# Ordering a DEPTH-2 encoder trunk by estimated times instead of counted half-chunk ticks

## The chip, the cores and the metric

The kernel runs on one core of one Trainium2 chip. The metric is device microseconds for one execution of the whole program, as the median of several executions.

## The reference

Two layers of a pre-norm encoder on 256 tokens of width 2048, all in fp32, batch 1. In each layer one input projection of the normalised stream feeds four branches, whose outputs are gated, lifted to 2048 columns, merged by sigmoid gates and passed through an output projection into a residual add:

```
h  = rmsnorm(x)                       # 256 x 2048
p  = h @ W_in                         # u, za, q/k/v and gates of each branch, 4 x 2048 merge gates
A  = s5(u): two scans (forward, backward) of 48 groups x 64 complex states,
     y = gelu(y);  y = y * sigmoid(y @ W_glu + b_glu)
B  = gated DeltaNet (bidirectional, chunks of 64, short convolution)
C  = grouped-query attention with 2-D rotary positions
M  = cross-attention into 256 memory tokens, rmsnorm(mem) @ W_km, W_vm
x  = x + (sum over br of sigmoid(gate_br) * ((br * silu(z_br)) @ W_br)) @ W_out
```

A final rmsnorm ends the trunk.

## The kernel before

**The weight stream.** All weights lie in `wpack` as chunks of 128 x 1024 fp32 (512 KB), 720 of them, in the order in which they are used. SP loads a chunk into `raw` (3 buffers), ACT rounds it to fp32r (`hi`, 3 buffers), DVE makes the rest, `lo` = `raw` - `hi` (3 buffers), and TensorE (PE) multiplies each with the activations, which are split in the same way, into `acc` (PSUM, 2 buffers). A chunk is 24 matmuls of 256 columns (kind T, `acc<-xT,hi`) or 12 of 512 columns (kind N, `acc<-hi,xT`). A run of chunks that fills one `acc` is a unit: `km`, `vm` (memory keys and values), `glu`, `out` and so on; `acts` are its activations (`xT` from the normalised stream, `memT` from memory, `sy` from the S5 output, `mT` from the merged branches).

**The branch work** (softmax, DeltaNet, the S5 scan, norms, transposes) is written as generators, called fibers. PE uses four PSUM tiles `bank` for it, and 13 tiles `scr` of 128 x 512 serve as scratch. Everything is emitted by one Python program and keeps that order on each engine: the order of emission is the order of execution. Nothing is reordered afterwards.

**What sets the order.** `run_unit` calls `tick` after each half chunk. A fiber yields the number of ticks to let pass before it goes on, for instance 6 between the issue of a load and its first use. `tick` runs fibers by rank while two counters of estimated backlog, one for DVE and one for ACT, are under `LIMIT`. The emptying of `acc` is put in `deferred` and is run first in a tick. Chunks are asked for by count: at the start of chunk n, `pump_split` emits `hi` and `lo` up to n+2, and `pump_raw` the loads up to n+4, whether a `raw` buffer is free by then or not; SP then waits at that load, with all later loads behind it.

**S5, where the prediction's terms lie.** `s5_fiber` has three stages in each layer. `chunk_sums` (12 blocks): 2 loads `scr<-Bd` of 256 KB each per block, which PE multiplies with `s5u`. A scan of 31 steps on DVE (`s5s`). `outputs` (12 blocks): 4 loads of 256 KB each per block, 2 `scr<-Wd` that DVE adds, and 2 `scr<-Cd` that go to PE with the sum. The result goes to DRAM (`Yd`), is read back as `s5y`, passes through gelu on ACT and DVE and is split into `sy`, which the `glu` units need. All these loads are on SP's queue, among the `raw` loads.

Helpers record the line of the helper: L240 is any ACT or DVE call, or a PE call on a `bank`; L418 is the stream's matmul, L372 the `raw` load.

Of the kernel before, what the change touches and what calls it, by code (L numbers as in the profile page):

```python
# [2 lines left out]

# [5 lines left out]
F32 = mybir.dt.float32  # L9
# [65 lines left out]
def layer_units(layer):  # L75
    """The weight stream of one layer, in the order in which the tensor engine takes it."""
# [78 lines left out]
def pack_small(inp):  # L155
    """Gains, biases and the like, per layer, one value or row per partition."""
# [20 lines left out]
def pack_s5(inp):  # L177
    """Per layer and partition (direction, state): a, log step, b and c; and d as diagonal blocks."""
# [12 lines left out]
def shape_consts():  # L191
    """Constants that follow from the shapes: identity, rotary angles, masks of the two directions."""
# [20 lines left out]
class Bank:  # L213
    """A set of equal tiles handed out and taken back in program order."""

    def __init__(self, tiles):
        self.free = list(tiles)

    def put(self, *tiles):
        self.free += tiles  # L220


class Meter:
# [5 lines left out]
    def __init__(self, eng, load, names, per, fixed):  # L229
        self._e, self._load, self._names, self._per, self._fixed = eng, load, names, per, fixed  # L230

    def __getattr__(self, name):
        f = getattr(self._e, name)

        def call(*args, **kw):
            o = kw.get("in_", kw.get("out", args[0] if args else None))
            if o is not None and name != "dma_start":
                for e in self._names:
                    self._load[e] += self._fixed + self._per * o.free_size()
            return f(*args, **kw)  # L240
        return call


class Builder:
    # microseconds of each engine per tick, and the backlogs between which the branches' work goes on
    DRAIN = {"V": 1.1, "S": 1}
    LIMIT = {"V": 2.125, "S": 2}
    FLOOR = {"V": 0.7, "S": 0.8}
    # memory attention, DeltaNet, attention and S5 by layer, and the preparation of S5
    RANK = ((3, 2, 4, 5), (5, 2, 4, 3))  # L250
    PREP_RANK = (3.5, 2.5)
    # ticks between the work of another engine and the tensor engine's use of it
# [46 lines left out]
    # A tick is half a chunk. A fiber yields the number of ticks to let pass before it goes on; 0 marks a place to pause.  # L299
    # Where an engine needs what another one makes, a tick in between keeps it from waiting for it in its queue.  # L300
    def spawn(self, gen, rank=None):
        """Of the fibers that can go on, the one with the lowest rank does; its own fibers get its rank."""
        self.fibers.append([self.tick_no, gen, self.rank if rank is None else rank])
        self.fibers.sort(key=lambda f: f[2])

    def wait(self, key):
        while key not in self.ready:
            yield 1

    def take(self, bank, n):  # L310
        while len(bank.free) < n:
            yield 1
        out, bank.free = bank.free[:n], bank.free[n:]
        return out
# [4 lines left out]
    def take_now(self, bank, n):  # L319
        while len(bank.free) < n:  # L320
            self.tick()
        out, bank.free = bank.free[:n], bank.free[n:]
        return out

    def tick(self):
# [3 lines left out]
        todo, self.deferred = self.deferred, []  # L329
        for due, f in todo:  # L330
            if due > self.tick_no:
                self.deferred.append((due, f))
                continue
            f = f() if callable(f) else f
            n = "end" if f is None else next(f, "end")
            if n != "end":
                self.deferred.append((self.tick_no + n, f))
        while all(self.load[e] < self.LIMIT[e] for e in self.load):
            f = next((f for f in self.fibers if f[0] <= self.tick_no), None)
            if f is None:  # L340
                break
            self.rank = f[2]
            try:
                f[0] = self.tick_no + next(f[1])
            except StopIteration:
                self.fibers.remove(f)
            self.rank = 0

    def need(self, key):
        guard = 0  # L350
        while key not in self.ready:
            self.tick()
            guard += 1
            assert guard < 100000, f"never ready: {key}"

# [1 line left out]
    def stream_setup(self):  # L357
# [18 lines left out]
    def pump_split(self, i):  # L376
        while self.next_split <= min(i, len(self.queue) - 1):
            n, w = self.next_split, self.queue[self.next_split]
            self.pump_raw(n)
            r = self.raw.pop(n)  # L380
            hi = self.hip.tile([128, CW], F32R, tag="hi", name="hi")
            lo = self.lop.tile([128, CW], F32R, tag="lo", name="lo")
            self.S.activation(out=hi[:, 0:w], in_=r[:, 0:w], func=AF.Copy)
            self.V.tensor_tensor(out=lo[:, 0:w], in0=r[:, 0:w], in1=hi[:, 0:w].bitcast(F32), op=ALU.subtract)
            self.split[n] = (hi, lo)
            self.next_split += 1

    def run_unit(self, u, act, nt=NT):
        """One unit of the stream: its product with the activations, in two banks of PSUM."""
        nc = self.nc  # L390
        acc = self.psa.tile([128, 2, 512], F32, tag="acc", name="acc")
        k = 0
        for j in range(u.nch):
            n = u.ch0 + j
            self.pump_split(n + self.AHEAD)
            self.pump_raw(n + self.AHEAD + 2)
            hi, lo = self.split.pop(n)
            todo, late, half = [], [], 6 if u.kind == "N" else 12
# [16 lines left out]
            todo += late  # L415
            for i, (kk, o, w, x, start, stop) in enumerate(todo):
                self.need(u.key + (kk // 4,))
                nc.tensor.matmul(o, w, x, start=start, stop=stop)  # L418
                if i == half - 1 or i == len(todo) - 1:
# [4 lines left out]
    def hi_lo(self, hi, lo, src, scale=None):  # L424
        """hi + lo = scale * src, each in the 12 bits that one pass of the tensor engine carries."""
# [8 lines left out]
    def hi_lo_later(self, *args):  # L434
        """hi_lo with a tick between the two engines."""
# [9 lines left out]
    def rsqrt(self, out, in_, mul, eps=EPS, p=-0.5):  # L445
        """out = (in_ * mul + eps) ** p on GpSimd, for a few columns."""
# [1180 lines left out]
```

## Time and profile before

| | us |
|---|---|
| median of 3 runs | 2333.71 |
| lowest and highest | 2330.08, 2336.09 |
| span of the profiled execution | 2329.0 |
| PE busy in it | 2261.9 (97%) |
| DVE, ACT busy | 1704.0 (73%), 1245.9 (53%) |
| DMA | 523.39 MB, mean 225 GB/s |

The span is that of one profiled execution. It lies 4.7 us under the median of the three runs. Of the span, PE sits idle for 2329.0 - 2261.9 = 67.1 us; a busy PE can still run at half its clock, which the column PEclk of the profile shows as a mean granted clock under 1.

### The profile page before, as it was taken

The page shows a single profiled execution, that of the slowest core. Times are in us where ns is not written, and L with a number is a line of the kernel's source. Part 1 is how long each engine was busy: PE and PEld are TensorE (multiplying, and loading weights), DVE is VectorE, ACT ScalarE, POOL GpSimd, SP SyncE. Part 2 cuts the span into 40 slices and gives each one's busy share as a digit, 9 for nine tenths or more (in the row PEclk, how much of TensorE's full clock was granted, in tenths as well). Part 3 has the DMA queues.
Part 4 walks back from the last instruction along what each step waited for, and adds up shares of the span by engine and source line. Part 5 has one row for each costly group of instructions (what it writes and reads, how often), then busy time and mean ns, then how long its engine had stood idle before and what let it go on. Part 6 is the DMA issues. An engine that isn't in the chain of part 4 may idle for free.

```text
span 2329.0 us, 38887 instructions
## 1 busy us (share of the span) xinstructions
PE 2261.9 (97%) x14684; PEld 1960.0 (84%) x14684; DVE 1704.0 (73%) x2824; ACT 1245.9 (53%) x2176; POOL 88.3 (4%) x153
## 2 busy tenths in 40 slices
PE   6999999999999999799999999999999999999997
PEld 6888978988988788697789987889888878888886
DVE  6788878858768955689688856888547895566564
ACT  6655564565564355555655554665646445554443
POOL 0000000000010000000000001000000000000000
PEclk9999999999999999999999999999999999999999
DMA  6677678745776488678776795656468558877674
GB/s 222 226 240 249 213 248 276 228 153 182 212 241 194 145 305 303 185 246 276 250 239 197 237 302 178 223 180 198 157 194 271 186 175 283 286 230 245 231 239 146
DMA packets 245133, 523.39 MB, mean 225 GB/s; under 512 B 59320, under 2 KB 111032, under 8 KB 244304
## 3 DMA queue, kind: packets, MB, share of 16 engines
q1 hardware_dynamic: 218400, 471.41, 63.1%
q10 hardware_dynamic: 21952, 36.80, 4.4%
q0 software_dynamic: 4592, 12.69, 1.6%
q8 instruction: 115, 1.88, 0.3%
q14 instruction: 74, 0.61, 0.1%
HBM read 468.21 MB, written 65.18 MB: 229 GB/s over the span
## 4 chain that ended last, share of the span: by engine, by line
PE 87%; DVE 5%; DMA 3%; ACT 3%; issue 1%; SPq 0%; ACTq 0%; POOL 0%; POOLq 0%; DVEq 0%
PE acc L418 78%; PE bank L240 9%; DVE lo L240 2%; DMA raw<-wpack 2%; ACT hi L240 1%; DVE scr L240 1%; DVE dnx L240 1%; ACT scr L240 0%; DVE s5s L240 0%; DMA xm<-x 0%; DMA s5y<-Yd 0%; SPq L1243 0%; ACT gt L240 0%; DMA oTA<-gt 0%; DMA Rb<-Rd 0%
## 5 line engine op out<-in xcount | busy, mean ns | idle before, releaser
L240 DVE TENSOR_TENSOR lo<-raw,hi 128x1024 fp32r<-128x1024 f32 (+1 forms) x720 | 873.5, 1216 | 528.1 <-ACT hi L240 512.5
L240 ACT ACTIVATE hi<-raw 128x1024 fp32r<-128x1024 f32 (+1 forms) x720 | 757.7, 1055 | 712.8 <-PE acc L418 368.6
L418 PE MATMUL acc<-hi,xT 128*128 128x512 f32 x2432 | 633.5, 398 | 3.0 <-ACT hi L240 2.4
L418 PEld LDWEIGHTS acc<-hi,xT 128*128 128x128 f32 x2432 | 447.0, 189 | 98.6 <-issue 5.6
L418 PE MATMUL acc<-xT,hi 128*128 128x256 f32 x3392 | 460.6, 287 | 8.1 <-DVE xT L240 5.6
L418 PEld LDWEIGHTS acc<-xT,hi 128*128 128x128 f32 x3392 | 427.6, 193 | 20.2 <-issue 8.4
L418 PE MATMUL acc<-lo,xT 128*128 128x512 f32 x1216 | 327.3, 391 | 2.6 <-DVE lo L240 2.5
L418 PEld LDWEIGHTS acc<-lo,xT 128*128 128x128 f32 x1216 | 228.2, 188 | 54.1 <-DVE lo L240 4.8
L418 PE MATMUL acc<-xT,lo 128*128 128x256 f32 x1696 | 238.8, 284 | 0.0
L418 PEld LDWEIGHTS acc<-xT,lo 128*128 128x128 f32 x1696 | 219.4, 192 | 0.1
L240 ACT ACTIVATE scr<-bank 128x128 f32<-128x128 f32 (+6 forms) x324 | 105.2, 335 | 140.9 <-PE bank L240 111.0
L418 PE MATMUL acc<-hi,y 128*128 128x512 f32 x640 | 163.2, 395 | 0.0
L418 PEld LDWEIGHTS acc<-hi,y 128*128 128x128 f32 x640 | 117.6, 188 | 25.3 <-issue 1.0
L418 PE MATMUL acc<-hi,mT 128*128 128x512 f32 x512 | 131.3, 397 | 0.0
L240 DVE TENSOR_TENSOR dnx<-dnx 32x30 f32<-32x30 f32 (+9 forms) x360 | 114.6, 318 | 10.4 <-DVE dnx L240 0.5
L418 PEld LDWEIGHTS acc<-hi,mT 128*128 128x128 f32 x512 | 95.3, 190 | 19.5 <-issue 0.4
L418 PE MATMUL acc<-lo,y 128*128 128x512 f32 x320 | 85.8, 390 | 0.0
L240 DVE TENSOR_TENSOR scr<-scr,scr 128x512 f32<-128x512 f32 (+4 forms) x132 | 77.4, 590 | 3.6 <-DMA scr<-s 1.1
L240 DVE SCALAR_TENSOR_TENSOR hT<-acc,small,hT 128x254 f32<-128x254 f32 (+1 forms) x144 | 69.3, 481 | 3.9
L418 PEld LDWEIGHTS acc<-lo,y 128*128 128x128 f32 x320 | 60.1, 188 | 12.8
L418 PE MATMUL acc<-lo,mT 128*128 128x512 f32 x256 | 68.6, 390 | 0.0
L240 PE MATMUL bank<-consts,scr 128*128 128x128 f32 x388 | 62.3, 274 | 5.3 <-DVE memT L240 5.2
(186 smaller groups left out, 2036.8 us busy)
## 6 DMA issues: line engine op xcount, KB each, us to landing
raw<-wpack SPq DMA_DIRECT2D x714, 512.0 KB, 4.2
Bd<-scr ACTq DMA_DIRECT2D x48, 256.0 KB, 4.4
Cd<-scr SPq DMA_DIRECT2D x48, 256.0 KB, 4.6
Wd<-Kd SPq DMA_DIRECT2D x32, 384.0 KB, 6.8
scr<-Bd SPq DMA_DIRECT2D x48, 256.0 KB, 5.5
scr<-Wd SPq DMA_DIRECT2D x48, 256.0 KB, 4.9
scr<-Cd SPq DMA_DIRECT2D x48, 256.0 KB, 5.5
Rb<-Rd SPq DMA_DIRECT2D x48, 128.0 KB, 4.5
```

The lines of the kernel that those rows point to most:

```text
L240: return f(*args, **kw)
L418: nc.tensor.matmul(o, w, x, start=start, stop=stop)
```

## The change

The counted ticks and the backlog counters go. A `Clock` keeps for each engine an estimated time at which it is free and, for each piece of a tile, when it was last written and read; each call is wrapped (`Engine`) and advances it by an estimated duration. Fibers go on when the estimated end of what they did last lies at least `MARGIN` before the estimated time of PE. `tick` is called after every 3 (N) or 6 (T) matmuls. Emptying `acc`, loading a `z` unit's branch output and loading its gate become fibers of rank -1. `raw` loads are emitted only when their buffer is estimated free, and `hi` and `lo` when their source is estimated there. The estimated landing of a load takes no account of other loads in flight: `dma` computes it from its own size only. The branch code itself (which instructions, which tiles, which queues) is unchanged, but for the words that declare a result ready.

```diff
 class Builder:
-    DRAIN = {"V": 1.1, "S": 1}
-    LIMIT = {"V": 2.125, "S": 2}
-    FLOOR = {"V": 0.7, "S": 0.8}
+    LIMIT = 2.0
+    LIMIT_EVAC = 4.0
+    MARGIN = 0.25
...
+    def dma(self, eng, out, in_):
...
+        kb = max(out.size(), 1) * 4 / 1024
+        self.t[eng] = dep + (0.5 if eng == "G" else 0.06)
+        land = dep + 2.0 + kb / 200.0
+        self.mark(land, W, R)
...
     def tick(self):
-        self.tick_no += 1
-        for e in self.load:
-            self.load[e] = max(-self.FLOOR[e], self.load[e] - self.DRAIN[e])
...
-        while all(self.load[e] < self.LIMIT[e] for e in self.load):
-            f = next((f for f in self.fibers if f[0] <= self.tick_no), None)
...
+        self.pump_raw(self.ahead, False)
+        self.splits()
+        seen = set()
+        while True:
+            now, back = self.time(), self.backlog()
+            f = next((f for f in self.fibers if f not in seen and f.t + self.MARGIN <= now
+                      and back < (self.LIMIT_EVAC if f.rank < 0 else self.LIMIT)), None)
+            if f is None:
+                return
+            self.cur, self.rank, self.clock.end = f, max(f.rank, 0), 0.0
+            n = next(f.gen, "end")
+            f.busy = max(f.busy, self.clock.end)
...
     def pump_raw(self, i, force=True):
         while self.next_raw <= min(i, len(self.queue) - 1):
+            old = self.next_raw - 3
+            if not force and (old in self.raw or self.gone.get(old, 0.0) > self.time() + 0.3):
+                return
...
+    def empty(self, u, acc, l, last):
+        if last is not None:
+            yield from self.wait(("emptied", last))
+        f = getattr(self, "evac_" + u.name)(u, acc, l)
+        if f is not None:
+            yield from f
+        u.emptied = True
+        yield 1
+        self.mark(("emptied", u))
```

How this moves instructions is read from the compiled order of both kernels. SP's queue at the S5 outputs of layer 0, before (`raw` is the weight stream; one row is one load, or several when it ends in a count):

```order
L372 DMA raw<-wpack 128x1024 x21
L1302 DMA scr_81<-Wd 128x512
L1303 DMA scr_87<-Wd 128x512
L1305 DMA scr_86<-Cd 128x512
L1305 DMA scr_91<-Cd 128x512
L372 DMA raw<-wpack 128x1024 x3
L1302 DMA scr_82<-Wd 128x512
L1303 DMA scr_80<-Wd 128x512
L1305 DMA scr_89<-Cd 128x512
L1305 DMA scr_79<-Cd 128x512
L372 DMA raw<-wpack 128x1024 x3
```

and after, at the same place (here and below L361 is the helper's line in place of L240 and L372):

```order
L361 DMA raw<-wpack 128x1024
L361 DMA scr_91<-Wd 128x512
L361 DMA scr_88<-Wd 128x512
L361 DMA scr_80<-Cd 128x512
L361 DMA scr_84<-Cd 128x512
L361 DMA raw<-wpack 128x1024
L361 DMA scr_81<-Wd 128x512
L361 DMA scr_85<-Wd 128x512
L361 DMA scr_90<-Cd 128x512
L361 DMA scr_79<-Cd 128x512
L361 DMA scr_87<-Wd 128x512
L361 DMA scr_80<-Wd 128x512
```

Before, 2 or 3 `raw` loads stand between the four loads of one block and those of the next; now there are 0 to 2. From the first `scr<-Wd` of the layer to the last `scr<-Cd`, 48 loads of 256 KB, there are 10 `raw` loads in all. The `chunk_sums` stage has the same: 24 loads `scr<-Bd` with 7 `raw` loads among them.

ACT at the S5 result `sy`, before; `gt<-acc,hbg` empties the first `glu` unit:

```order
L240 ACTIVATE scr_80<-s5y 128x512
L240 ACTIVATE scr_84<-scr_84 128x512
L240 ACTIVATE scr_83<-scr_83 128x512
L240 ACTIVATE scr_80<-scr_80 128x512
L240 ACTIVATE sy<-s5y 128x2x256 x3
L1057 DMA scr_90<-s 128x144
L240 ACTIVATE hi<-raw 128x1024
L240 ACTIVATE hi<-raw 128x512
L240 ACTIVATE hi<-raw 128x1024
L240 ACTIVATE gt<-acc,hbg 128x256 x2
```

and after:

```order
L361 ACTIVATE hi<-raw 128x1024
L361 ACTIVATE sy<-s5y 128x2x256
L361 ACTIVATE scr_84<-scr_84 128x512
L361 ACTIVATE sy<-s5y 128x2x256
L361 ACTIVATE gt<-acc 128x512
L361 ACTIVATE hi<-raw 128x1024 x2
L361 ACTIVATE y<-gt 128x2x256
L361 ACTIVATE sy<-s5y 128x2x256
L361 ACTIVATE hi<-raw 128x1024 x2
```

Before, three `hi` splits stand between `sy` and the first emptying of a `glu` unit. After, more than twenty do: `sy` is made while the units ahead of `glu` still run.

POOL at the start of layer 1's memory, before:

```order
L1532 DMA xm<-x 128x2x512 x4
L535 DMA memtok<-mem 128x2048 x2
L1190 MEMSET scr_82 128x256
L1549 DMA x_97<-xm 128x2x512
L448 TENSOR_SCALAR nstat<-nstat 128x2
```

and after:

```order
L361 DMA xm<-x 128x2x512 x4
L361 DMA x_97<-xm 128x2x512
L361 DMA memtok<-mem 128x2048 x2
L361 MEMSET scr_84 128x256
L361 TENSOR_SCALAR nstat<-nstat 128x2
```

The load of `memtok` now stands behind a store of the first finished columns of `x`, and its user on ACT follows three chunks of PE work later, where before it was four.

## Rows read from the trace of the kernel before

**Rows 1.** The page: busy time of each engine, and the chain that ended last.
```profile
PE 2261.9 (97%) x14684; PEld 1960.0 (84%) x14684; DVE 1704.0 (73%) x2824; ACT 1245.9 (53%) x2176; POOL 88.3 (4%) x153
...
PE 87%; DVE 5%; DMA 3%; ACT 3%; issue 1%; SPq 0%; ACTq 0%; POOL 0%; POOLq 0%; DVEq 0%
```

**Rows 2.** By 50 us: busy us (count) of PE, PEld, DVE, ACT, POOL; PEclk, DMA share, GB/s.
```profile
0.00:50.00 50.00, 30.80 (x214) 29.46 (x215) 33.10 (x88) 31.23 (x62) 1.10 (x6) 0.93 0.63 223
50.00:100.00 50.00, 47.10 (x296) 42.17 (x296) 37.19 (x56) 34.27 (x65) 1.41 (x4) 0.97 0.73 239
...
750.00:800.00 50.00, 45.17 (x315) 35.83 (x313) 47.43 (x125) 19.57 (x34) 0.00 (x0) 0.97 0.45 144
900.00:950.00 50.00, 44.35 (x256) 35.12 (x254) 30.34 (x37) 22.18 (x32) 0.00 (x0) 0.99 0.90 284
950.00:1000.00 50.00, 43.22 (x241) 37.37 (x242) 35.57 (x79) 31.79 (x50) 1.82 (x3) 0.91 0.54 172
1050.00:1100.00 50.00, 47.81 (x253) 39.01 (x252) 44.90 (x62) 23.70 (x40) 1.76 (x3) 1.00 0.80 270
1100.00:1150.00 50.00, 47.62 (x237) 38.47 (x236) 34.03 (x53) 30.63 (x61) 4.50 (x8) 0.97 0.81 278
1900.00:1950.00 50.00, 47.40 (x330) 38.73 (x329) 38.78 (x84) 23.58 (x49) 2.11 (x2) 0.97 0.60 203
```

**Rows 3.** PE's timeline at the stalls: start, us, group [idle before it <-releaser].
```profile
787.65 1.23 PE L240 MATMUL bank<-dnx,scr 128*128 128x128 f32 x8 [2.29 <-DVE scr L240]
788.57 3.67 PE L418 MATMUL acc<-hi,xT 128*128 128x512 f32 x8
...
954.01 0.58 PE L418 MATMUL acc<-sy,hi 128*128 128x256 f32 x1 [9.66 <-ACT sy L240]
...
1099.72 0.65 PE L240 MATMUL bank<-consts,xm 128*128 128x128 f32 x4 [2.19 <-DVE mT L240]
```

**Rows 4.** PE's timeline where nothing interrupts the stream, kind T, then N.
```profile
101.49 1.12 PE L418 MATMUL acc<-memT,lo 128*128 128x256 f32 x8
...
104.37 1.12 PE L418 MATMUL acc<-memT,lo 128*128 128x256 f32 x8
...
145.49 1.98 PE L418 MATMUL acc<-hi,memT 128*128 128x512 f32 x8
...
148.21 1.98 PE L418 MATMUL acc<-hi,xT 128*128 128x512 f32 x8
```

**Rows 5.** ACT's timeline at the S5 result, then a row of DVE's.
```profile
953.33 1.83 ACT L240 ACTIVATE sy<-s5y 128x512 fp32r<-128x512 f32 x3
...
940.21 0.16 DVE L240 TENSOR_SCALAR hbg<-small 128x6 f32<-128x6 f32 x1
```

**Rows 6.** DMA issues of the whole run: KB each, median us to landing.
```profile
scr<-Wd SPq DMA_DIRECT2D x48, 256.0 KB, 4.9
scr<-Cd SPq DMA_DIRECT2D x48, 256.0 KB, 5.5
...
memtok<-mem POOLq DMA_DIRECT2D x2, 1024.0 KB, 11.4
...
dnz<-Xd SPq DMA_DIRECT2D x48, 16.0 KB, 1.8
```

**Rows 7.** DMA of 840 to 940 us, the S5 outputs of layer 0.
```profile
raw<-wpack SPq DMA_DIRECT2D x30, 512.0 KB, 5.2
scr<-Wd SPq DMA_DIRECT2D x18, 256.0 KB, 5.1
```

**Rows 8.** As rows 2: stretches in which the DMA engines are full or nearly so.
```profile
910.00:920.00 10.00, 10.00 (x66) 7.84 (x65) 5.55 (x6) 5.74 (x9) 0.00 (x0) 1.00 1.02 393
1110.00:1120.00 10.00, 10.00 (x60) 7.92 (x59) 5.92 (x8) 2.82 (x7) 0.00 (x0) 1.00 1.00 398
1740.00:1750.00 10.00, 9.84 (x81) 7.45 (x81) 6.00 (x9) 3.79 (x5) 0.00 (x0) 1.00 1.03 386
...
1350.00:1400.00 50.00, 50.00 (x264) 42.87 (x263) 25.83 (x36) 28.37 (x49) 0.96 (x1) 1.00 0.91 301
```

More of the change, by code (lines that the diff above doesn't have):

```diff
@@ L213, with __init__ @@
 class Bank:
-    def __init__(self, tiles):
-        self.free = list(tiles)
+    def __init__(self, clock, tiles):
+        self.clock = clock
+        self.free = [(0.0, i, t) for i, t in enumerate(tiles)]
+        self.n = len(self.free)
     def put(self, *tiles):
[L220 to L233, printed above, removed]
-        def call(*args, **kw):
[L236 to L240, printed above, removed]
-        return call
+        for t in tiles:
+            self.n += 1
+            self.free.append((self.clock.last(t), self.n, t))
+        self.free.sort(key=lambda f: f[:2])
@@ L301, in spawn, with time, mark @@
     def spawn(self, gen, rank=None):
-        self.fibers.append([self.tick_no, gen, self.rank if rank is None else rank])
-        self.fibers.sort(key=lambda f: f[2])
+        f = Fiber(gen, self.rank if rank is None else rank)
+        if self.cur:
+            f.t = max(self.clock.end, self.cur.busy)
+        self.fibers.append(f)
+        self.fibers.sort(key=lambda f: f.rank)
+    def time(self):
+        self.now = max(self.now, self.clock.t["PE"])
+        return self.now
+    def mark(self, key):
+        t = max(self.clock.end, self.cur.busy if self.cur else 0.0)
+        self.ready[key] = max(self.ready.get(key, 0.0), t)
@@ L306, in wait, with there @@
+    def there(self, key):
+        return key in self.ready and self.ready[key] + self.MARGIN <= self.time()
     def wait(self, key):
-        while key not in self.ready:
-            yield 1
+        while not self.there(key):
+            yield POLL
     def take(self, bank, n):
[L311 to L314, printed above, removed]
+        while True:
+            out = bank.take(n, self.time() + 0.3)
+            if out is not None:
+                return out
+            yield POLL
@@ L349, in need, with backlog, tick @@
-    def need(self, key):
[L350 to L354, printed above, removed]
+    def backlog(self):
+        return max(self.clock.t["V"], self.clock.t["S"]) - self.time()
+    def tick(self):
+        self.pump_raw(self.ahead, False)
+        self.splits()
+        seen = set()
+        while True:
+            now, back = self.time(), self.backlog()
[6 more added lines that the diff above has]
+            f.busy = max(f.busy, self.clock.end)
+            self.cur, self.rank = None, 0
+            if n == "end":
+                self.fibers.remove(f)
+            elif n == POLL:
+                seen.add(f)
+            elif n:
+                f.t, f.busy = max(f.t, f.busy), 0.0
@@ L357, in stream_setup, with idle @@
+    def idle(self, test):
+        guard = 0
+        while not test():
+            self.tick()
+            if test():
+                break
+            self.now = self.time() + 0.25
+            guard += 1
+            assert guard < 20000, "never ready"
+    def need(self, key):
+        if not self.there(key):
+            self.idle(lambda: self.there(key))
     def stream_setup(self):
@@ L379, in pump_split, with splits @@
             self.pump_raw(n)
[L380 to L385, printed above, removed]
-            self.next_split += 1
+            self.pending += [(n, "S", w), (n, "V", w)]
+            self.next_split += 1
+    def splits(self, upto=-1):
+        while self.pending:
+            n, e, w = self.pending[0]
+            r = self.raw[n]
+            src = r if e == "S" else self.split[n][0]
+            if n > upto and self.clock.written(src) > max(self.time(), self.clock.t[e]) + 0.1:
+                return
+            self.pending.pop(0)
+            if e == "S":
+                hi = self.hip.tile([128, CW], F32R, tag="hi", name="hi")
+                self.S.activation(out=hi[:, 0:w], in_=r[:, 0:w], func=AF.Copy)
+                self.split[n] = [hi]
+            else:
+                lo = self.lop.tile([128, CW], F32R, tag="lo", name="lo")
+                hi = self.split[n][0]
+                self.V.tensor_tensor(out=lo[:, 0:w], in0=r[:, 0:w], in1=hi[:, 0:w].bitcast(F32), op=ALU.subtract)
+                self.split[n].append(lo)
+                self.gone[n] = self.clock.t["V"]
+                del self.raw[n]
     def run_unit(self, u, act, nt=NT):
-        nc = self.nc
         acc = self.psa.tile([128, 2, 512], F32, tag="acc", name="acc")
@@ L394, in run_unit @@
             n = u.ch0 + j
+            self.splits(n + 1)
             self.pump_split(n + self.AHEAD)
-            self.pump_raw(n + self.AHEAD + 2)
+            self.ahead = n + self.AHEAD + 2
             hi, lo = self.split.pop(n)
-            todo, late, half = [], [], 6 if u.kind == "N" else 12
+            todo, late = [], []
             for kk in range(min(u.kpc, u.nk - k)):
@@ L415, in run_unit @@
             todo += late
+            part = 3 if u.kind == "N" else 6
             for i, (kk, o, w, x, start, stop) in enumerate(todo):
                 self.need(u.key + (kk // 4,))
-                nc.tensor.matmul(o, w, x, start=start, stop=stop)
-                if i == half - 1 or i == len(todo) - 1:
+                self.PE.matmul(o, w, x, start=start, stop=stop)
+                if i % part == part - 1 or i == len(todo) - 1:
                     self.tick()
@@ L609, in done @@
     def done(self, key):
-        self.count[key] = self.count.get(key, 0) - 1
-        if self.count[key] <= 0:
-            self.ready.add(key)
+        n = self.count[key] = self.count.get(key, 0) - 1
+        t = self.late[key] = max(self.late.get(key, 0.0), self.clock.end, self.cur.busy)
+        if n <= 0:
+            self.ready[key] = t
     def expect(self, key, n):
@@ L787, in evac_dqkv @@
         tiles = []
+        if u.idx and u.idx % 3 == 0:
+            yield from self.wait(("hfree", l, u.idx // 3 - 1))
         for i in range(2):
@@ L1482, in evac_zm @@
                 self.acts[("y" + br, l)] = [self.y[:, 0:4], self.y[:, 4:8]]
+        yield from self.wait(("o", u))
         z = acc[:, :, 0:256]
@@ L1508, in evac_prod @@
         stored = u.br in self.gd
+        yield from self.wait(("gate", u) if stored else ("cqT", l))
         for t in range(NT) if stored else (slice(0, NT),):
@@ L1594, in build @@
             self.layer(l)
-        self.need("end")
-        while self.fibers:
-            self.tick()
+        self.idle(lambda: "end" in self.ready and not self.fibers)
 def emit(tc, a, out):
```

259 lines of the change are left out of this document (189 added, 70 removed).

## The prediction, made before the changed kernel ran

> **What bounds the kernel now.** I read the page first: PE is busy for 97% of the span, and it makes up 87% of the chain that ended last [rows 1]. PE's own work is the same in both kernels, so the change can only win or lose in the 67 us in which PE is idle, in the stretches in which it is busy at half its clock (1.2 of 2.4 GHz), and in new waits. Next I cut the span into stretches of 50 us. Nearly all show 50.00 us of PE at clock 1.00; those that don't, the start and the end apart, are in [rows 2]. Their idle time (50 less PE busy) is 2.90 + 4.83 + 5.65 + 6.78 + 2.19 + 2.38 + 2.60 = 27.3 us, without the first stretch. Their mean clock gives 50 x (1 - PEclk) = 1.5 + 1.5 + 0.5 + 4.5 + 1.5 + 1.5 = 11.0 us more. Some of that is counted twice, since the clock was low while PE stood idle around 950 us: I take 2 off. So 36 us lie in seven stretches. The first stretch has 19.2 us of idle time, of which some 13 pass before the first matmul; I leave it out.
>
> The timeline of PE says what these are [rows 3]. PE stood still for 9.66 us before 954.01 because ACT had not made `sy`. At 787.65 it waited 2.29 us for a `scr` of DVE, at 1099.72 it waited 2.19 us for `mT`. After the wait at 787.65, eight matmuls of 512 columns took 3.67 us, where eight take 1.98 at full clock [rows 4]: another 1.7 us lost. The wait at 1099.72 cost no clock (1050 to 1100 us has 1.00).
>
> **What the change removes.** All these are cases where another engine got its work at the last moment. (1) `sy`: today ACT makes it at 953.33 [rows 5], with `glu` next on PE. In the new order it stands more than twenty `hi` splits earlier, some 60 us at 2.7 to 2.9 us per chunk (two `lo` groups of kind T start 2.88 us apart, two `hi` groups of kind N 2.72 [rows 4]). So the 900 to 1000 us part, 12.4 idle and 5.0 clock less the 2 counted twice, 15.4 us, should go whole. (2) `memT`, `mT` and the DeltaNet waits, 20.5 us: emptying of PSUM is tried every quarter chunk and the products are spread over more chunks. I take them as gone. Together **-36 us**. If only (1) goes, it is -15.
>
> **What it moves, and what that costs.** The S5 loads. Today the outputs stage lies over some 100 us, and its 18 `scr<-Wd` (9 blocks) go with 30 `raw` loads in 840 to 940 us [rows 7]. In the new order the 48 loads of 256 KB of a layer have only 10 `raw` of 512 KB among them: 12.6 + 5.2 = 17.8 MB. PE's work in that time: 10 chunks of 2.8 us are 28 us. The blocks' own matmuls: from 850 to 950 us about 94 us of PE (50.00 and 44.35 [rows 2]) hold some 30 chunks, 84 us, which leaves 10 for 9 blocks and other branch work, 0.75 to 1.1 each; twelve are 9 to 13. So 37 to 41 us, I take 39: 456 GB/s are asked for. Likewise `chunk_sums`: 24 loads and 7 `raw`, 10.0 MB, in 7 x 2.88 us and some 3 us of small matmuls, 23.5 us: 424 GB/s. What the DMA engines gave when they had no free share is 386 to 398 [rows 8]. The difference must come out of PE's time, since `scr<-Cd` and `scr<-Bd` go straight into matmuls, and `scr<-Wd` into a DVE add with `lo` splits queued behind it. Two things more. A load lands late even alone: `dnz<-Xd`, with 16 KB, takes 1.8 us [rows 6], so 2 us per stage pass before the first data. And the change plans a load of 256 KB with 2.0 + 256/200 = 3.3 us, while such loads take 4.9 to 5.5 today [rows 6].
>
> Cost per layer, with rate r in GB/us: (17.8/r - 39 + 2) + (10.0/r - 23.5 + 2) = 27.8/r - 58.5. At 397 GB/s this is 11.5 us, both layers **+23 us**. Its ends: 0, if the `raw`, `hi` and `lo` buffers (9 chunks of 512 KB) and early issue absorb it; and 68 us at 301 GB/s, what a stretch of 50 us with share 0.91 gave [rows 8]. I take 397 since a full queue is the nearest case.
>
> The Trainium skill (DMA: Bandwidth & Descriptors, section Bandwidth) puts the limit for HBM loads at about 358 GB/s for a core when both cores of a pair stream, and reports 425 for one core alone with 16 MB. By 358 the loads would cost 38 us, by 425 14. The rows above, 386 to 398 over ten microseconds, lie between the two, so I keep the rows.
>
> Half clock. New waits of PE of around 2 us may be followed by a stretch at half clock, as at 787.65; 1.5 us for each of the four S5 stages, **+6** (0 if they come singly, as at 1099.72; 14 if twice per stage).
>
> `memtok`: its load takes 11.4 us [rows 6]. In the new order ACT's first use follows three chunks of PE work later, 8 us, and the `hi` splits stand behind that instruction on ACT, with PE behind them: **+3.4** (0 if the splits that are ahead cover it, 5 with a lost clock).
>
> Start: DVE gets some 13 small S5 instructions ahead of the first `xT` product for which PE waits; at 0.16 us for a small one [rows 5], **+2** (0 to 3).
>
> The rest is put at nothing: the instruction counts are the same, the scan's DVE work is spread instead of packed, and the emptying that may now run later than today is covered by the second `acc`; if that cover fails, a unit waits some 1 us.
>
> Sum: -36 + 23 + 6 + 3.4 + 2 = -1.6. Against the profile's 2329.0 us that is 2327.4, and with the 4.7 us by which the median of the runs lies above that span, **2332 us**.
>
> **The rivals.**
>
> *The loads are absorbed* (chance 0.32). SP now gets to a `scr` load without having waited at a `raw` whose buffer isn't free, so the loads may start earlier than their place says, and PE has up to three split chunks in hand. For it: today no S5 load holds PE up. Against: the loads need `scr` buffers that free only as PE consumes them, and a `Cd` that is late stops PE whatever else is in hand. Loads 0 to 10 us, no clock lost: -36 + 5 + 5.4 = -26, 2308; without any cost at all 2298.
>
> *The loads cost more and the kernel gets slower* (chance 0.20). Loads and `raw` share the engines with stores and with `gates` loads, and the rate is that of a longer stretch: [rows 8] have 301 GB/s over 50 us. At 340 the loads cost 27.8/0.340 - 58.5 = 23.3 us per layer, 47 in all, and the sum is -36 + 47 + 11.4 = +22, 2356. At 301 it is 2377. The point from which it decides: with 11.4 us of other costs the sum is zero at 12.3 us per layer, which is 393 GB/s, and the kernel is 7 us slower at 374.
>
> *The stalls don't go* (chance 0.08). The order follows estimates; where a DVE instruction takes longer, or a queue stands, work still comes late, and only `sy` and a few others are gone: -18 in place of -36, 2350.
>
> **How the numbers follow.** My forecast, that the stalls go and the S5 loads take the gain back, has 0.40; its own range is 2318 to 2346, from 386 to 413 GB/s and some 2 us either way per stage. A difference of 0.3%, 7 us, is about what this measurement can tell from none. Of the forecast's 0.40, 0.12 lie under 2327, 0.20 within, 0.08 over 2341. The absorbed loads give 0.32 faster, the slow loads 0.20 slower, the stalls that stay 0.07 slower and 0.01 same. So faster 0.44, same 0.21, slower 0.35. The range goes from 2296, no cost at all, to 2362, the slow loads at about 332 GB/s: some 0.07 lie below, 0.10 above.
>
> **What would show it.** Right: PE's wait for `sy` gone from the timeline; in four stretches of 25 to 50 us (the S5 sums and outputs of both layers) PE busy well below 50 with releasers DMA `scr<-Cd`, DMA `scr<-Bd` or DVE `scr` and `lo`, and a DMA share near 1.0 there; landing of `scr<-Wd` and `scr<-Cd` above 6 us. Wrong: PE at 50.00 in those stretches (the loads were absorbed), or a DMA share well under 1 with PE waiting all the same (then it is the delay of each load, not the rate). The sum is wrong most of all if the PE time of the outputs stage is not the 39 us that I counted: two us more or less there are 4 us of the result.

## The result, and the profile after

| | us | ratio to before, 95% interval |
|---|---|---|
| before, median | 2334.90 (2330.08 to 2338.44) | |
| changed, median | 2355.78 (2352.34 to 2363.83) | 1.0099 [1.0077, 1.0122] |
| changed, second chip use (`e10_again` below) | 2353.43 (2350.75 to 2354.72) | 1.0093 [1.0076, 1.011] |

The change made the kernel 21 us slower. The profile of the changed kernel is that of its slowest execution (2363.83 us, span 2362.1), the profile of before that of its fastest (2330.08, span 2329.0), so the two spans differ by 33.1 us. The second profile of the changed kernel, span 2351.9, is nearer to the median, and I give its sums beside the first one's.

The page: busy time, the chain by engine, and the chain by line (against [rows 1]).

```profile
PE 2277.5 (96%) x14684; PEld 1968.6 (83%) x14684; DVE 1704.1 (72%) x2824; ACT 1243.5 (53%) x2176; POOL 89.8 (4%) x153
...
PE 65%; DMA 7%; issue 4%; DVE 3%; ACT 2%; SPq 2%; POOL 0%; ACTq 0%; POOLq 0%; DVEq 0%
PE acc L361 58%; PE bank L361 7%; DMA raw<-wpack 3%; DMA scr<-Wd 2%; SPq L361 2%; DVE lo L361 1%; ACT hi L361 1%; DVE scr L361 1%; ACT scr L361 1%; DMA scr<-Bd 1%; DMA memtok<-mem 1%; DVE hT L361 0%; DVE xm L361 0%; DMA Xd<-dnx 0%; DMA dnz<-Xd 0%
```

Before, DMA had 3% of the chain and SP's queue nothing. Now DMA has 7%, SP's own issuing 2%. The stretches of 50 us in which PE isn't busy at full clock (columns as in [rows 2]; left out are the start, the end, and four stretches with 1.1 us or less of idle time):

```profile
50.00:100.00 50.00, 47.38 (x304) 41.90 (x303) 40.98 (x62) 35.26 (x66) 1.46 (x4) 1.00 0.72 241
...
400.00:450.00 50.00, 44.94 (x447) 42.71 (x447) 35.49 (x63) 26.31 (x62) 1.42 (x2) 0.93 0.57 184
550.00:600.00 50.00, 47.56 (x339) 38.06 (x338) 28.11 (x54) 24.59 (x52) 1.94 (x3) 0.93 0.48 151
600.00:650.00 50.00, 46.47 (x342) 38.59 (x340) 25.71 (x35) 22.85 (x38) 0.00 (x0) 1.00 0.95 248
750.00:800.00 50.00, 48.84 (x316) 39.45 (x315) 46.23 (x99) 21.70 (x29) 0.52 (x1) 1.00 0.59 187
800.00:850.00 50.00, 44.45 (x388) 34.79 (x388) 26.79 (x46) 27.57 (x67) 1.41 (x2) 0.97 0.87 301
850.00:900.00 50.00, 47.34 (x362) 40.69 (x362) 24.76 (x29) 24.66 (x39) 0.00 (x0) 0.97 0.77 242
950.00:1000.00 50.00, 47.83 (x272) 41.67 (x271) 45.23 (x62) 25.76 (x40) 0.63 (x2) 0.97 0.74 238
1250.00:1300.00 50.00, 46.52 (x325) 43.83 (x324) 33.26 (x53) 25.43 (x33) 1.15 (x2) 0.97 0.90 286
1650.00:1700.00 50.00, 46.20 (x330) 37.07 (x329) 25.14 (x40) 24.25 (x49) 1.94 (x3) 0.93 0.51 155
1750.00:1800.00 50.00, 46.81 (x392) 39.19 (x391) 21.92 (x32) 27.02 (x55) 0.00 (x0) 0.97 0.86 269
1950.00:2000.00 50.00, 42.42 (x395) 31.25 (x388) 20.68 (x25) 25.29 (x62) 1.36 (x2) 0.93 0.90 317
2000.00:2050.00 50.00, 46.93 (x259) 39.93 (x260) 29.26 (x33) 25.49 (x32) 0.00 (x0) 0.97 0.72 215
```

Read as in the prediction (50 less PE busy, and 50 x (1 - PEclk)), they fall into three groups. The S5 stages (600, 800, 850, 1750, 1950, 2000): 25.6 us idle and 9.5 of clock. Stretches 400, 550 and 1650, which showed nothing before: 11.3 and 10.5. The rest, 50, 750, 950 and 1250: 9.4 and 3.0. The main waits in them, on PE's timeline (columns as in [rows 3]):

```profile
412.86 0.50 PE L361 MATMUL bank<-scr,scr 32*32 32x32 f32 x32 [2.50 <-ACT scr L361]
...
569.46 0.53 PE L361 MATMUL bank<-scr,UA 32*32 32x32 f32 x16 [2.32 <-ACT scr L361]
...
841.87 0.66 PE L361 MATMUL bank<-scr,scr 128*32 128x128 f32 x16 [3.68 <-ACT scr L361]
...
975.04 3.37 PE L361 MATMUL acc<-sy,hi 128*128 128x256 f32 x16 [2.17 <-DVE scr L361]
...
1286.23 3.62 PE L361 MATMUL acc<-xT,hi 128*128 128x256 f32 x16 [2.09 <-ACT hi L361]
...
1659.61 0.42 PE L361 MATMUL bank<-scr,UA 32*32 32x32 f32 x16 [2.77 <-ACT scr L361]
...
1978.53 1.08 PE L361 MATMUL bank<-scr,scr 128*32 128x128 f32 x16 [5.45 <-ACT scr L361]
```

The 9.66 us before `sy` are gone; 2.17 us are left at 975. The waits at 412, 569 and 1659 are DeltaNet's (`UA` is its matrix). They are named after ACT, but ACT isn't the cause. All engines around 402 us:

```profile
402.45 3.67 SPq L361 DMA_DIRECT2D dnz<-Xd  x8
...
406.13 0.63 ACT L361 ACTIVATE scr<-dnz 128x512 f32<-128x512 f32 x1 [2.14 <-DMA dnz<-Xd]
...
406.81 1.05 SPq L361 DMA_DIRECT2D raw<-wpack  x2
...
411.64 1.06 ACT L361 ACTIVATE hi<-raw 128x1024 fp32r<-128x1024 f32 x1 [2.52 <-DMA raw<-wpack]
```

SP needs 3.67 us to issue eight loads of 16 KB, 0.46 us each. The plan books 0.06. So `scr<-dnz` is late on ACT, and the `raw` load behind the burst is too, with the next `hi`, and behind that `hi`, in ACT's order, the copy of `bank` to `scr` for which PE waits at 412.86.

In the S5 outputs the first to be late is DVE's add (SP's issues, then DVE, then ACT behind it; PE's wait is the one at 841.87 above):

```profile
826.54 4.96 SPq L361 DMA_DIRECT2D raw<-wpack  x2
...
834.49 0.79 SPq L361 DMA_DIRECT2D scr<-Wd  x2
...
840.24 1.29 DVE L361 TENSOR_TENSOR scr<-scr,scr 128x512 f32<-128x512 f32 x2 [4.02 <-DMA scr<-Wd]
840.96 1.73 ACT L361 ACTIVATE scr<-s5s 64x256 f32<-64x256 f32 x4 [6.00 <-DVE scr L361]
```

The same kernel's DMA engines before, in and after this wait, and over the whole stage (first `scr<-Wd` to last `scr<-Cd`), columns as in [rows 8]:

```profile
830.00:832.00 2.00, 2.00 (x47) 1.40 (x43) 1.13 (x1) 1.91 (x4) 0.00 (x0) 1.00 0.26 95
...
838.00:842.00 4.00, 0.32 (x5) 0.13 (x8) 1.29 (x2) 0.99 (x3) 0.00 (x0) 1.00 1.03 389
840.00:850.00 10.00, 8.13 (x91) 5.98 (x92) 4.86 (x6) 6.55 (x15) 0.00 (x0) 0.83 1.04 400
...
804.70:860.30 55.60, 47.68 (x428) 36.48 (x428) 25.04 (x37) 29.41 (x72) 1.41 (x2) 0.94 0.90 314
```

DVE idles 4.02 us for `scr<-Wd` with `lo` queued behind; the DMA engines are full (1.03, 389 GB/s) while PE waits. But the rate is not the whole of it. Before that, at the second of the two `raw` loads, SP stood 4.2 us for a buffer that `lo` had not freed, with the S5 loads behind it, and the engines ran nearly empty (0.26, 95 GB/s in 830 to 832). SP's own waits over the stage, the two longest in total (us in total, times, longest us):

```profile
SPq L361 <- DVE lo L361: 13.0, 6, 4.3
SPq L361 <- PE bank L361: 7.0, 6, 2.1
```

And at 1286 SP is again held, by `Wd<-Kd` loads for the S5 preparation:

```profile
1264.71 6.68 SPq L361 DMA_DIRECT2D Wd<-Kd  x5
1271.49 1.00 SPq L361 DMA_DIRECT2D raw<-wpack  x1
1272.54 5.91 SPq L361 DMA_DIRECT2D Wd<-Kd  x4
1278.55 1.48 SPq L361 DMA_DIRECT2D raw<-wpack  x2
...
1285.12 1.06 ACT L361 ACTIVATE hi<-raw 128x1024 fp32r<-128x1024 f32 x1 [5.88 <-DMA raw<-wpack]
```

Nine loads take SP 12.6 us, with one `raw` among them. A `Wd<-Kd` load holds SP 0.55 us in the median of all 32; here it is 1.4 us in the mean, and the DMA engines are full:

```profile
1264.00:1286.00 22.00, 18.75 (x153) 18.11 (x151) 11.90 (x23) 10.33 (x14) 1.15 (x2) 1.00 1.05 328
```

How much of this wait is issuing and how much the rate isn't shown: `e1_issue` and `e3_rate` below both take most of it away (0.6 and 1.3 us idle in that stretch, against 3.5).

### The profile page after: what moved, and what is told of

The parts are those of the page before. It is cut to its first block, busy times and chain, and to the rows that moved or that the text cites. A ratio compares the mean times of both kernels' runs of the same rounds, so it can differ in the third digit from the quotient of the medians.

```text
span 2362.1 us, 38879 instructions
## 1 busy us (share of the span) xinstructions
PE 2277.5 (96%) x14684; PEld 1968.6 (83%) x14684; DVE 1704.1 (72%) x2824; ACT 1243.5 (53%) x2176; POOL 89.8 (4%) x153
## 4 chain that ended last, share of the span: by engine, by line
PE 65%; DMA 7%; issue 4%; DVE 3%; ACT 2%; SPq 2%; POOL 0%; ACTq 0%; POOLq 0%; DVEq 0%
PE acc L361 58%; PE bank L361 7%; DMA raw<-wpack 3%; DMA scr<-Wd 2%; SPq L361 2%; DVE lo L361 1%; ACT hi L361 1%; DVE scr L361 1%; ACT scr L361 1%; DMA scr<-Bd 1%; DMA memtok<-mem 1%; DVE hT L361 0%; DVE xm L361 0%; DMA Xd<-dnx 0%; DMA dnz<-Xd 0%
## 5 line engine op out<-in xcount | busy, mean ns | idle before, releaser
L361 DVE TENSOR_TENSOR lo<-raw,hi 128x1024 fp32r<-128x1024 f32 (+1 forms) x720 | 873.5, 1216 | 459.5 <-ACT hi L361 449.9
L361 ACT ACTIVATE hi<-raw 128x1024 fp32r<-128x1024 f32 (+1 forms) x720 | 759.1, 1056 | 773.3 <-PE acc L361 480.1
L361 PE MATMUL acc<-hi,xT 128*128 128x512 f32 x2432 | 630.7, 397 | 2.5 <-ACT hi L361 2.5
L361 PEld LDWEIGHTS acc<-hi,xT 128*128 128x128 f32 x2432 | 451.2, 190 | 98.2 <-issue 5.6
L361 PE MATMUL acc<-xT,hi 128*128 128x256 f32 x3392 | 459.5, 287 | 11.8 <-DVE xT L361 5.5
L361 PEld LDWEIGHTS acc<-xT,hi 128*128 128x128 f32 x3392 | 430.9, 194 | 21.5 <-DVE xT L361 6.4
L361 PE MATMUL acc<-lo,xT 128*128 128x512 f32 x1216 | 341.0, 396 | 0.0
L361 PEld LDWEIGHTS acc<-lo,xT 128*128 128x128 f32 x1216 | 227.0, 190 | 49.1 <-issue 2.6
L361 PE MATMUL acc<-xT,lo 128*128 128x256 f32 x1696 | 247.5, 286 | 0.0
L361 PEld LDWEIGHTS acc<-xT,lo 128*128 128x128 f32 x1696 | 222.6, 193 | 3.4 <-issue 3.3
L361 ACT ACTIVATE scr<-bank 128x128 f32<-128x128 f32 (+6 forms) x324 | 104.4, 333 | 136.7 <-PE bank L361 104.9
L361 PE MATMUL acc<-hi,y 128*128 128x512 f32 x640 | 160.9, 392 | 0.0
L361 PEld LDWEIGHTS acc<-hi,y 128*128 128x128 f32 x640 | 118.7, 188 | 24.6 <-issue 0.4
L361 PE MATMUL acc<-hi,mT 128*128 128x512 f32 x512 | 128.8, 393 | 0.1
L361 DVE TENSOR_TENSOR dnx<-dnx 32x30 f32<-32x30 f32 (+9 forms) x360 | 114.5, 318 | 13.3 <-DMA dnx<-Sd 3.1
L361 PEld LDWEIGHTS acc<-hi,mT 128*128 128x128 f32 x512 | 95.0, 188 | 20.4 <-issue 0.6
L361 DVE TENSOR_TENSOR scr<-scr,scr 128x512 f32<-128x512 f32 (+4 forms) x132 | 77.4, 591 | 33.8 <-DMA scr<-Wd 31.1
L361 PE MATMUL acc<-lo,y 128*128 128x512 f32 x320 | 88.3, 393 | 0.0
L361 PE MATMUL bank<-consts,scr 128*128 128x128 f32 x388 | 65.2, 280 | 7.2 <-ACT scr L361 4.1
L361 DVE SCALAR_TENSOR_TENSOR hT<-acc,small,hT 128x254 f32<-128x254 f32 (+1 forms) x144 | 69.1, 481 | 3.9
L361 PE MATMUL acc<-lo,mT 128*128 128x512 f32 x256 | 70.5, 393 | 0.9 <-DVE lo L361 0.9
L361 PEld LDWEIGHTS acc<-lo,y 128*128 128x128 f32 x320 | 59.3, 188 | 12.3 <-issue 0.4
```

What stands on the lines that cost most here:

```text
L361: o = f(*args, **kw)
```

## The experiments

Two theories, and a variant of the second. **Theory 1**: SP's issue time, booked as 0.06 us, makes bursts late. **Theory 3**: the DMA engines' rate; the plan lets every load land as if alone. **Theory 2**: each load simply takes longer than booked. Most experiments change only what the plan books, so that the order changes and the instructions don't; `e7_split`, `e8_pool` and `e13_dnzsplit` keep the changed kernel's order and change the loads. In the table, "DeltaNet" and "S5" are idle time plus lost clock of PE, from the 50 us stretches 400, 450, 550, 1600, 1650 and 600, 650, 800, 850, 1700, 1750, 1900, 1950, 2000 (which hold other branch work too; waits too short to show as idle are not in it, and one that a new order moves out of these stretches isn't either).

| | median us | ratio, 95% interval | DeltaNet us | S5 us |
|---|---|---|---|---|
| before | | | 0.3 | 4.3 |
| changed | 2355.78 | 1.0099 [1.0077, 1.0122] | 21.8 | 35.8 |
| e10_again | 2353.43 | 1.0093 [1.0076, 1.011] | 22.7 | 29.7 |
| e1_issue | 2317.92 | 0.9938 [0.9916, 0.9961] | 1.5 | 12.5 |
| e2_land | 2336.54 | 1.0015 [1.0, 1.003] | 11.6 | 13.7 |
| e3_rate | 2313.18 | 0.9923 [0.9905, 0.9941] | 10.7 | 1.3 |
| e4_all | 2325.81 | 0.9976 [0.9963, 0.9989] | 0.2 | 10.8 |
| e5_dnz | 2344.05 | 1.0059 [1.0044, 1.0074] | 8.5 | 38.4 |
| e6_s5 | 2348.34 | 1.0089 [1.0069, 1.0109] | 17.1 | 14.5 |
| e7_split | 2382.33 | 1.022 [1.0196, 1.0244] | 22.4 | 57.7 |
| e8_pool | 2361.30 | 1.0139 [1.0123, 1.0156] | 21.8 | 32.5 |
| e9_both | 2309.47 | 0.991 [0.9892, 0.9928] | 11.5 | 6.6 |
| e11_pipe480 | 2330.57 | 0.9994 [0.9981, 1.0006] | 15.6 | 16.9 |
| e12_pipe330 | 2315.56 | 0.9934 [0.9916, 0.9952] | 13.3 | 6.0 |
| e13_dnzsplit | 2376.55 | 1.0195 [1.0176, 1.0214] | 36.2 | 36.9 |
| e14_raw | 2353.37 | 1.0099 [1.0082, 1.0116] | 10.6 | 33.4 |
| e15_dnz_s5 | 2332.13 | 0.9995 [0.9981, 1.0008] | 4.1 | 17.3 |

**e1_issue.**

```diff
-        self.t[eng] = dep + (0.5 if eng == "G" else 0.06)
+        self.t[eng] = dep + 0.5
```

> The changed kernel with one number of its Clock altered: a DMA issue on SP and ACT is booked with 0.5 us instead of 0.06 (the trace of the changed kernel has 3.65 us for eight dnz<-Xd issues in a row). Theory 1 (issue time): DeltaNet's bursts of eight dnz loads were planned to land together and come 3 to 4 us late. Then the waits before bank<-scr,UA near 412, 569 and 1659 us go, with the half clock behind them, some 20 us, and a few us of the S5 waits: 2330 to 2338. Theories 2 and 3 (landing time or shared rate of the S5 loads): the S5 waits stay, and the DeltaNet waits have another cause: 2350 to 2358.

One number turns 1.0% slower into 0.6% faster, more than any theory said. DeltaNet's waits are gone and some 60% of S5's too. For S5 this doesn't tell issuing from rate: 0.5 us booked for each load of 256 KB is a limit of 512 KB/us, close to the pipe of `e11_pipe480`, which leaves about as much (16.9 against 12.5).

**e2_land.**

```diff
-        land = dep + 2.0 + kb / 200.0
+        land = dep + (2.0 + kb / 200.0 if eng == "SP" and kb > 384 else 2.0 + kb / 75.0 if eng == "SP" else 2.0 + kb / 110.0)
```

> The changed kernel with the landing time of its Clock altered for loads other than raw: 2.0 us + KB/75 on SP (5.4 for 256 KB instead of 3.3), KB/110 on ACT and POOL (11.3 for 1 MB instead of 7.1). Theory 2 (each load lands later than planned): the S5 waits (about 24 us of PE idle time with 8 or 9 us of half clock) and the wait for memtok go: 2320 to 2332. Theory 3 (rate): the loads are only asked for earlier at the start of each stage, the rate asked for stays, half of the S5 waits stay: 2338 to 2346. Theory 1: S5 and DeltaNet waits stay: 2350 to 2358.

Between theories 2 and 3: over half of the S5 waits go, not all.

**e3_rate**, and with other rates **e11_pipe480** and **e12_pipe330**.

```diff
-        land = dep + 2.0 + kb / 200.0
+        self.pipe = max(self.pipe, dep) + kb / 390.0
+        land = max(dep + 2.0 + kb / 200.0, self.pipe + 2.0)
```

> The changed kernel with one shared pipe of 390 KB/us in its Clock: a load lands no sooner than 2.0 us after all that was issued before it has passed at that rate; a lone load is booked as before. Theory 3 (shared rate): the S5 stages are stretched and their waits go: 2320 to 2332. Theory 2: the stages are stretched a little, each load still comes 2 us late: 2340 to 2350. Theory 1: 2350 to 2358.

> As e3_rate, with a pipe of 480 instead of 390 KB/us, above what any stretch of a trace here has shown. Theory 3 (rate of the DMA engines): the S5 waits come back in part, 2318 to 2332. If it is enough to put any order into the bursts, and the rate itself doesn't matter: as e3_rate, 2311 to 2318.

> As e3_rate, with a pipe of 330 KB/us, under what the engines give. Theory 3: no S5 waits are left to remove, the stages only get longer; 2310 to 2318, unless sy in layer 0 comes so late that glu waits. If the engines give less than 390 in these stages: faster than e3_rate by 3 us or more.

S5 loses 1.3 us with 390, 16.9 with 480, and 6.0 with 330: with a pipe wider than the engines the waits come back, a narrower one gains nothing more. So the rate booked matters, not just any order in the bursts. `e3_rate` came out faster than any theory said. Its S5 outputs of layer 0:

```profile
787.20:847.60 60.40, 60.02 (x494) 46.59 (x493) 29.38 (x38) 35.78 (x77) 1.42 (x2) 1.00 0.90 318
```

The stage takes 60.4 us instead of 55.6 (first `scr<-Wd` to last `scr<-Cd`: 787.16 to 847.54 us here, 804.71 to 860.30 in the changed kernel), at nearly the same rate, 318 against 314 GB/s. There are 15 `raw` loads among its 48, not 10, so PE has more stream work in that time and is busy for all but 0.4 of 60.4 us. That alone isn't enough: `e11_pipe480` has 15 there too, and waits.

**e4_all**: the three edits together.

> All three numbers together: issue 0.5 us, later landing, shared pipe. If all the new waits come from what the Clock books for DMA, the S5, DeltaNet and memtok waits go and what the change removed stays removed: 2300 to 2315, faster than before. If the waits come from elsewhere (order of ranks, PSUM banks, ACT's queue): 2335 or more. The S5 result is made later here, close to the first glu unit; if it comes too late, the wait for sy returns in layer 0, some 10 us: 2315 to 2325.

Slower than `e1_issue` or `e3_rate` alone. DeltaNet is clean (0.2), but other waits have come up, among them 3.05 us at 914 and 2.89 at 1242, and the booked delays put `sy` next to `glu` again. My sum of "all repaired" was wrong; that booking too much costs as well is what these waits suggest, not a thing tried by itself.

**e5_dnz** and **e6_s5**: the edit of `e1_issue` for `dnz` alone, and for `Bd`, `Wd`, `Cd` alone.

> The changed kernel, with an SP issue booked as 0.5 us for the loads of dnz alone. Theory 1 (the bursts of eight dnz issues make DeltaNet's waits): the waits before bank<-scr,UA near 412, 569 and 1659 us go, the S5 waits stay: 2356 - 20 = 2336, between 2330 and 2342. If those waits come from something else that the later order of e1_issue cured by chance: 2350 to 2358.

> The changed kernel, with an SP issue booked as 0.5 us for the loads of Bd, Wd and Cd alone. The DeltaNet waits stay, the S5 waits fall by about two thirds (24 us idle and 9 us of half clock to some 10): 2356 - 22 = 2334, between 2328 and 2342. The two parts, e5_dnz and e6_s5, should add up to about the 38 us of e1_issue.

Each did what it should in its own place, 21.8 or 22.7 to 8.5 us for DeltaNet and 30 to 36 to 14.5 for S5. The time followed only in part for `e5_dnz` (0.4%) and hardly for `e6_s5` (0.1%, inside the intervals); both missed their ranges. The DeltaNet column falls in other runs too (10.6 in `e14_raw`, 10.7 in `e3_rate`), since a late load can hold something else. A better measure is how long ACT and DVE idle for `dnz` data over the whole run (us, times), here of before, of the changed kernel, of `e5_dnz` and of `e13_dnzsplit` below:

```profile
  DMA dnz<-Xd: 1.4, 1
...
  DMA dnz<-Xd: 25.7, 17
...
  DMA dnz<-Xd: 7.2, 7
...
  DMA dnz<-Xd: 75.5, 23
```

In every run that books the issue of `dnz` it is 1.5 to 9.7 us; in all other variants of the changed kernel with eight loads to a burst it is 19.7 to 35.7.

**e7_split** (each S5 load as two halves) and **e8_pool** (`Cd` from POOL's queue), in the changed kernel's own order.

```diff
+            if op == "dma_start" and kw["in_"].tensor.name[:2] in ("Bd", "Wd", "Cd") and kw["out"].tensor.name[:3] == "scr":
+                for i in range(2):
+                    o = f(out=kw["out"][:, 256 * i:256 * i + 256], in_=kw["in_"][:, 256 * i:256 * i + 256])
...
+            if op == "dma_start" and kw["in_"].tensor.name[:2] == "Cd" and kw["out"].tensor.name[:3] == "scr":
+                o = self.pool.dma_start(**kw)
```

> The changed kernel in its own order, with each S5 load of 256 KB cut into two issues of 128 KB: same bytes, twice the issues (144 more on SP in the four S5 stages, about 0.45 us each). If SP's issue time is what holds the S5 stages (theory 1), their waits grow by 20 us or more per layer where the queue is the limit: 2385 to 2410. If the rate of the DMA engines is the limit (theory 3), the issues lie in its shadow: 2352 to 2368.

> The changed kernel in its own order, with the 48 loads of Cd issued by POOL instead of SP: same bytes, 24 issues fewer on SP in each outputs stage. Theory 1: the waits of the outputs stages (18 us idle, 8 of half clock) shrink by half or more: 2335 to 2345. Theory 3 (rate): no gain, 2350 to 2360, or more if POOL's loads land later than SP's.

Twice the issues cost 1.2% (2382 us lies between the two expectations); taking two fifths of the issues (24 of 58) off SP in the outputs stage gains nothing and costs 0.4%, as theory 3 allows (`scr<-Cd` lands in 6.3 us from POOL, 5.5 from SP, which may hide a gain). In the changed kernel the 58 issues, at 0.46 us, are 27 us of a stage of 56, so SP's issuing isn't what fills it; twice the S5 issues are 49 us, and in `e7_split` the stage takes 65.8. With `Cd` off its queue SP only stands longer in that stage, 21.9 us for `lo` and 12.7 for PE's `bank`, against 13.0 and 7.0. So in S5 the rate comes before issuing. How much of its waits comes from SP standing at a `raw` load, with S5 loads behind it, no run has separated.

**e9_both**: `e1_issue` and `e3_rate` together.

> The changed kernel with the shared pipe of 390 KB/us (as e3_rate) and an SP issue of 0.5 us (as e1_issue), the landing formula left alone. If the new waits have these two causes, DeltaNet by the bursts on SP and S5 by the rate, nearly nothing but the start stays: 2302 to 2312, faster than e3_rate. If the two are the same cause counted twice: no faster than e3_rate, 2311 to 2318.

The fastest version, 20.7 us under before (2330.19 on that chip). It can't be told from `e3_rate`: 0.991 [0.9892, 0.9928] and 0.9923 [0.9905, 0.9941].

**e10_again**: no edit.

> The changed kernel itself once more, on the same chip as the others of this call, for a second profile: 2345 to 2358 here, with waits of PE in the same places as in the first profile (DeltaNet near 412, 569 and 1659 us, S5 near 640, 840, 1775 and 1980). If those waits were chance, they lie elsewhere.

As expected; the waits lie in the same places.

**e13_dnzsplit**: each `dnz` load as two of 16 partitions, in the changed kernel's order.

> The changed kernel in its own order, with each of the eight dnz loads cut into two issues: same 128 KB, 16 issues in a row on SP instead of 8, some 3.7 us more per burst, six bursts. Theory 1 (the burst of issues makes DeltaNet's waits): the waits near 412, 569 and 1659 us grow by 2 to 4 us each, with half clock behind them, and bursts that were covered start to show: 2362 to 2378, against 2345 to 2356 for the changed kernel itself. If those waits have another cause (the landing of Xd, ACT's queue): 2347 to 2358.

Its SP, PE at the same place as 402 to 413 above, and PE at the bursts of the waits at 569 and 1659:

```profile
404.29 7.37 SPq L363 DMA_DIRECT2D dnz<-Xd  x16
...
410.12 0.45 PE L365 MATMUL bank<-scr,UA 32*32 32x32 f32 x16 [2.51 <-ACT scr L365]
418.68 0.50 PE L365 MATMUL bank<-scr,scr 32*32 32x32 f32 x32 [3.56 <-ACT scr L365]
...
578.11 0.41 PE L365 MATMUL bank<-scr,UA 32*32 32x32 f32 x16 [4.11 <-ACT scr L365]
581.88 0.91 PE L365 MATMUL bank<-scr,UA 32*32 32x32 f32 x16 [1.88 <-ACT scr L365]
...
1676.94 0.45 PE L365 MATMUL bank<-scr,UA 32*32 32x32 f32 x16 [2.98 <-ACT scr L365]
1682.05 0.56 PE L365 MATMUL bank<-scr,UA 32*32 32x32 f32 x16 [3.36 <-ACT scr L365]
```

The same bytes in twice the issues: 7.37 us of SP instead of 3.67, and the waits at all three places grow. Each load lands no later (1.7 us in the median; 2.4 and 1.8 in the two profiles of the changed kernel), so it is the issuing. Theory 1 holds for DeltaNet.

**e14_raw** and **e15_dnz_s5**: the edit of `e1_issue` for `raw` alone, and for `dnz` and the S5 loads.

> The changed kernel, with 0.5 us booked for the issue of raw loads alone. If the raw loads' share of SP's time is what e1_issue had beyond e5_dnz and e6_s5 (1.61% against 0.40% and 0.10%): 2320 to 2332. If it is only the sum of dnz and S5 loads that does it: 2345 to 2356.

> The changed kernel, with 0.5 us booked for the issues of dnz, Bd, Wd and Cd together, not for raw. If the two parts add up as single runs did: 2338 to 2344. If they need each other (a wait that is taken away in one place only moves while the other place stays late): 2318 to 2330.

`raw` alone does nothing for the time (a new wait of 4.98 us for `hi` stands at 340.80, outside both columns). The two parts together give 1.0%, about twice their single sum (0.4% and 0.1%, each to some 0.2%), so they seem to need each other; 2332 us lies between the two expectations; `e1_issue` has 0.6% more, from the loads that are left (`Wd<-Kd`, gates, stores) or from those with `raw`. Which, wasn't tried.

## Why the prediction was wrong

The forecast was 2332 us, within 0.3% of before; it came out 21 us slower, inside the range, and on the side that I gave 0.35. By its steps:

1. **The stalls go, -36.** Right in mechanism, the size somewhat less. In the stretches of [rows 2], 38.3 us stood; the changed kernel has 2.6 at 50, 1.2 at 750, 3.7 at 950 and nothing to speak of at 900, 1050, 1100 and 1900: about 30 us are gone. The 2.17 us left at 975 are for a `scr` of DVE.
2. **S5 loads, +23, and half clock, +6.** 25.6 and 9.5 us in the first profile, 21.2 and 8.5 in the second: the place is right and the size nearly, and the rate is the best supported reason (`e3_rate`, `e11_pipe480`, `e12_pipe330`). But the size was luck: two inputs were off and cancelled. The stage of layer 0 holds 48 us of busy PE, not 39, since other branch work is laid into it, and the engines gave 314 GB/s over it, not 397. 400 was reached over ten microseconds only, as in [rows 8]. Of the signs, PE was well below 50 in the four stages and the engines were full at waits, but not over the stage (0.90), landing stayed at 5.2 to 5.7 us instead of above 6, and SP did stand at `raw` loads without a free buffer, which the rival with the absorbed loads had assumed to be over.
3. **`memtok`, +3.4.** Next to nothing. The load is issued at 1138.32 and read at 1149.43 us; PE's only wait near it is 0.90 us at 1159.60, for a `lo` that stands behind the scaling of `memtok` on DVE.
4. **Start, +2.** PE is busy for 30.11 us of the first 50, against 30.80; with the clock at 0.97 instead of 0.93 nothing is lost.
5. **"The rest is put at nothing."** This step failed. DeltaNet lost 21.8 us (22.7 in the second profile) where before had 0.3, and the stretch with the `Wd<-Kd` loads 5.0 at 1250 (3.5 idle, 1.5 clock; 2.8 in the second profile). I counted instructions and DMA bytes, and priced what SP does between two loads only as a rate in bytes. The eight `dnz` loads are 0.13 MB, but 3.67 us of SP. The order of before hid them: its burst started at 442.88 and took 4.56 us, and ACT's first `scr<-dnz` stood so late in the order that it came at 449.64, 6.8 us after the start, with no wait of PE:

```profile
442.88 4.56 SPq L914 DMA_DIRECT2D dnz<-Xd  x8
...
449.64 1.14 ACT L240 ACTIVATE scr<-dnz 128x512 f32<-128x512 f32 x2
```

In the new order it comes 3.7 us after the start (402.45, 406.13), having waited for it. `e5_dnz` and `e13_dnzsplit` show this from both sides.

Summed: -30 + 35 + 22 + 5 - 1 = 31, against 33.1 between the two profiles. The rival that came nearest, slow S5 loads with 2356, had the time by accident: its 47 us for the loads were 30 to 36, and DeltaNet made up the difference. (The upper end of the range, 2362, goes with 327 GB/s by the prediction's own formula, not 332.)

The Trainium skill (DMA: Bandwidth & Descriptors, section Anatomy of one DMA — SWDGE (gpsimd) path) lists sequencer dispatch with about 50 ns, near what the plan books; that section is on loads issued by POOL. No run here shows so short a hold: this trace has SP held for 0.46 us by each `dnz` load, and POOL for 0.55 us by a `Sd<-scr` store of the same 16 KB.

## What to carry to other kernels

A planner that orders work by estimates needs a price for every resource that queues: here the issuing engine (0.5 us for a load instead of 0.06) and the shared DMA rate were missing, and putting the two in turned 1% slower into 0.9% faster without touching an instruction of the branches (the rate alone gave 0.8%, the issue alone 0.6%). When an order gets tighter, look first at bursts of small loads on one queue: bytes don't show them, the issuing engine's timeline does. And a wait named after ACT or DVE may start at a load two steps back, or at a load that stands behind a burst.

## What was not expected of the hardware

- SP was held 0.46 us for a load of 16 KB (3.67 us for eight), about as long for one of 256 KB (0.79 us for two), and 0.55 us for a `Wd<-Kd` load in the median of 32, but up to 2.10 us for one while the engines were full (share 1.05 in 1264 to 1286).
- Over the S5 outputs of layer 0 the DMA engines moved 314 GB/s in the changed kernel, where PE waited, and 318 in `e3_rate`, where it didn't, both at a busy share of 0.90. The most for such a stage was 345 at 0.96 (`e1_issue`, layer 1), and 400 over ten microseconds.
- Waits of 2.3 to 2.8 us of PE (569.46, 1659.61) stood in stretches whose mean granted clock fell to 0.93, 3.5 us of 50: more than the waits themselves. That isn't always so: the wait of 1.80 us at 638.08 cost no clock (1.00 in 600 to 650), nor did one of 3.12 us at 842.12 in `e14_raw` (1.00 in 800 to 850).
